# Four gate projections as a double of a seven-product stage, in place of plain chunks ahead of it, with the operand combinations built over half as many steps

## The chip, the cores and the metric

The kernel runs on one core of a Trainium2 chip. A core has a matrix engine (PE, with a separate row PEld for the loading of stationary weights), a vector engine (DVE), a scalar engine (ACT), GpSimd (POOL) and the sync engine (SP), which here only issues transfers. The metric is the device time of one execution in microseconds, as the median of repeated runs. What can be told from no change in this kernel is a difference of about 0.2%, some 2.5 us.

## The reference

One encoder layer on x (512 tokens by 1024 features, float32): a half-step SwiGLU feed-forward, a mixer, and a second half-step feed-forward, each behind an RMSNorm. The mixer projects the normalised input h once and cuts the product apart:

```python
proj = h @ w_in                                   # 1024 x 7936
pa, pq, pk, pv, pg = ...                          # pa: q, k, v of 24 dilated heads; pg: 2 x 1024 gate columns
o_a = dilated attention(pa); o_b = grouped-query attention with rotary(pq, pk, pv)
gates = jax.nn.sigmoid((pg + b_gate).reshape(B, S, N_BRANCHES, D))
merged = gates[:, :, 0] * (o_a @ w_branch_a) + gates[:, :, 1] * (o_b @ w_branch_b)
return merged @ w_out
```

The change touches the first 512 of the 2048 columns of `pg`: four of sixteen gate chunks of 128 columns.

## The kernel before

**Products.** Everything is held feature-major: a tile has 128 features (partitions) by 512 tokens. Each float32 operand is split into a high and a low part in a reduced float32 format (`hH`, `hL` for the normalised input, `wh`, `wl` for weights), and each product is three matmuls (`mm3`, lines 249 to 251: high by high, high by low, low by high). A weight chunk is 128x1024 floats (512 KB): SP loads it raw (`wr`, `wa`, `wt`), ACT rounds it to `wh` (line 234), DVE subtracts to get `wl` (line 235). The rings are short: three `wh`/`wl` pairs, and a fourth (`whx`) for the stage and down-projection items whose index in the order is 3 modulo 4, while a stage pool is open.

**Plain chunks.** `feat` (a gate or a plain q/k chunk) multiplies one weight chunk with all of h: 8 blocks by 3 matmuls, each 512 tokens wide. `token` (the v projections) keeps h stationary and streams the weights. When a gate chunk ends, DVE scales it by the norm factor `R` (line 687) and SP stores it to DRAM (`gate_d`, line 688); it is read back much later, beside the branch products.

**The seven-product stage.** `strassen` takes four chunks at a time (a "double", chunks f and f+1 with both parts) and computes their product with h as a 2x2 block product in seven block products in place of eight. The steps are A11, S1, S2, A12, S3, S4, A22; each is 24 matmuls 256 tokens wide. The right-hand operands of A11, A12 and, in the mixer, S4 are halves of h itself; those of S1, S3, A22 and S2 are combinations of quarters of x that are built beforehand into `TQH`/`TQL` by `tq_steps`: twelve small steps (`put`, `sums`, `part` for each of four k), with two ACT scalings, four DVE combinations of 128x256, one ACT cast (line 734) and one DVE subtraction (line 735) per k. On the weight side A11, A12 (tag `wa`) and A22 (`wr`) are loaded as they are; S1 and S3 (`wt`) are loaded by SP and a second block is added to them by an accumulating transfer from POOL's queue (line 216); S2 and S4 (`ws`) are added by DVE (line 233). Successive doubles overlap by one another's steps: the steps of f+2 begin before those of f end.

**Order around the change.** The PE program order is written out by hand, by `self.items` and the hooks of `project_qk`; on the other engines a scheduler orders the instructions, so they need not stand in the order of the code. The mixer opens with the v projection of group 1 (4 chunks, 32 steps of the generator), then four gate chunks (8 steps each, 64 in all), with the norm statistics at steps 7, 12 and 17 and the twelve `tq_steps` at steps 12, 16, ..., 56. Then comes the stage: five doubles of q/k chunks, whose results go to DRAM (`qk_d`) by POOL's queue, and a sixth double that computes the v projection of group 0. After the stage come the v projection of group 2 and the other plain chunks, woven into the attention; the attention begins by reading q and k back on POOL's queue (`fetch`, line 711).

**Offsets.** Weight tiles of the seven-product steps start at 160 or 32 bytes modulo 256, by the parity of the item's index (`offset`): `return 160 - 128 * (n % 2)`.

Of the kernel before, what the change touches and what calls it, by code (L numbers as in the profile page):

```python
# [20 lines left out]
EARLY, EARLIER = 4, 6  # L21
GROUPS = {"a": (4, 8, 16, 22), "b": (2, 8, 16, 22)}
PAIRS = ((0, 0), (1, 0), (0, 1), (0, 2), (1, 1), (1, 2), (2, 0), (3, 0), (2, 1), (2, 2), (3, 1), (3, 2))
NSQ = 10
STEPS = ("A11", "S1", "S2", "A12", "S3", "S4", "A22")
# [44 lines left out]
class Layer:  # L70
    def __init__(self, ctx, tc, a):
# [27 lines left out]
        gates = lambda lo, hi: [("g", j) for j in range(lo, hi)]  # L99
        self.items = ([("v", 1)] + gates(0, 4) + [("sw", 0), ("v", 2)] + gates(4, 6) + [("qk", f) for f in range(NSQ, 12)]  # L100
                      + gates(6, 13) + [("b", g) for g in range(3)] + gates(13, 16) + [("pa", 0)])
# [3 lines left out]
        for kind, n in self.items:  # L105
            if kind == "sw":
                self.order += [("swq", at) for at in self.slots(range(0, NSQ + 2, 2))]
                continue
            name, m = span[kind]
            self.order += [(name, m * n + i) for i in range(m)]  # L110
        self.order += [(name, i) for name in ("wpb", "wo") for i in range(8)]
        self.order += self.ffn_order("b")
        self.raws, self.tiles, self.used, self.wx, self.TQ = {}, [], 0, None, None
        self.cap = len(self.order)
# [5 lines left out]
    def turn_of(self, n):  # L120
        if self.kind[n] != "wt":
            return n
        s, f = self.order[n][0][2], self.order[n][1][0]
        return n - (EARLIER if s != "q" and f >= GROUPS[s][1] else EARLY)

# [34 lines left out]
    def ring(self, tag, n, done, last):  # L160
        held, bufs = self.rings[tag], BUFS[tag]
        pool = self.wb if tag in ("wr", "wh") else self.wx
        if pool is None or (len(held) >= bufs and held[-bufs] >= done):
            return None
        held.append(last)
        if tag[:2] != "wh":
            return pool.tile([128, 1024], F32, tag=tag, name=tag, bufs=bufs)
        at = (self.offset(n) - BASE[tag]) % 256 // 4
        return tuple(pool.tile([128, 1088], F32R, tag=t, name=t, bufs=bufs)[:, at:at + 1024] for t in ("wh", "wl"))
# [18 lines left out]
    def load(self, n):  # L188
# [17 lines left out]
        def part(q):  # L206
            if name[2] == "q" and f == NSQ:
                return self.a["wav0"][2 * int(q[1]) + int(q[2]) - 3].rearrange("p (a c) -> p a c", a=2)
            i, c = 2 * f + int(q[1]) - 1, 512 * (int(q[2]) - 1)
            return w[i:i + 3:2, :, c:c + 512].rearrange("a p c -> p a c")  # L210

# [89 lines left out]
    def strassen(self, s, fs, evict):  # L301
        st, order = {}, self.slots(fs)
        end = self.used + len(order) - 1
        for f, step in order:
# [7 lines left out]
            for j in range(2):  # L312
                for k in range(4):
                    ops = self.right(step, k)
                    if s == "q" and f == NSQ:
                        ops = [t[:, 128 * j:128 * j + 128] for t in ops] + [t[:, 256 * k:256 * k + 256] for t in cur]
                    else:
                        ops = [t[:, 512 * j + 128 * k:512 * j + 128 * k + 128] for t in cur] + list(ops)
                    self.mm3(ps[:, 256 * j:256 * j + 256], *ops, fresh and j == 0 and k == 0, k == 3, not (fresh and j == 0))
# [115 lines left out]
    def ffn(self, s, gin, gnext, hooks, out=None, side=None):  # L435
        with ExitStack() as ctx:
            pool = lambda n, **k: ctx.enter_context(self.tc.tile_pool(name=n, reuse_waits="tile", **k))
            tp = pool("hT", bufs=1, side="right")
            self.TH = tp.tile([128, 3, 4, 256], F32R, name="TH")
            self.TL = tp.tile([128, 3, 4, 256], F32R, name="TL")  # L440
            self.wx = self.shifted(pool("wx", bufs=1), 128)
            self.cp = self.shifted(pool("c", bufs=2), 128)
            self.ffn_run(s, gin, gnext, hooks, out, side or {}, pool("g", bufs=1))
            self.wx = None
# [294 lines left out]
    def project_qk(self):  # L739
        nc, tc = self.nc, self.tc  # L740
        with ExitStack() as ctx:
            pool = lambda n, **k: ctx.enter_context(tc.tile_pool(name=n, reuse_waits="tile", **k))
            tp = self.shifted(pool("qT", bufs=1), 64)
            self.TQ = [tp.tile([128, 4, 4, 256], F32R, name=f"TQ{c}") for c in "HL"]
            self.wx = self.shifted(pool("wxq", bufs=1), 64)
            cp, qp = pool("cq", bufs=2), pool("qo", bufs=2)
            steps = self.tq_steps(cp)
            hooks = {7: self.stat_r, 12: self.stat_R, 17: self.stat_p}
            for n, _ in enumerate(self.stream(self.items[:self.head])):
                if n in hooks:  # L750
                    hooks[n]()
                if n > 8 and n % 4 == 0 and steps:
                    steps.pop(0)()
# [17 lines left out]
            def store(f, part, t):  # L771
                i = 2 * f + part
                nc.gpsimd.dma_start(self.qk_d[i:i + 3:2].rearrange("c p n -> p c n"), t.rearrange("p (c n) -> p c n", c=2))

# [9 lines left out]
            def evict(f, step, ps):  # L784
# [15 lines left out]
                elif step == "S4":  # L800
                    nc.vector.tensor_add(hi, ps, hi)
                    if f == NSQ:
                        tokens(lo, 0, slice(0, 256), False)
# [5 lines left out]
                    store(f, 0, o)  # L809
                elif f == NSQ:  # L810
                    tokens(ps, 0, slice(256, 512), True)
# [6 lines left out]

            for _ in self.strassen("q", range(0, NSQ + 2, 2), evict):
                pass  # L820
# [498 lines left out]
```

## Time and profile before

| | |
|---|---|
| median of 3 runs | 1253.38 us (1253.02 to 1253.86) |
| the profiled execution | 1252.48 us |
| its span, first to last instruction | 1250.7 us |
| matmul busy (PE) | 1239.0 us, 99% |
| weight loads (PEld) | 1112.9 us, 89% |
| DVE, ACT, POOL busy | 891.4, 595.6, 122.6 us |
| moved by DMA | 183.49 MB, 147 GB/s |
| granted TensorE clock | 0.998 |

The times of the trace are counted from the first instruction of the span; the profiled execution is 1.8 us longer than its span and 0.9 us under the median of the runs. A busy PE is not a PE at its peak, since matmuls are pipelined: the distance from one start to the next tells the pace. The mixer's head (the v projection of group 1 and the four gates) lies between about 348 and 393.5 us, the stage between 393.5 and 508.7 us.

### The profile page before, as it was taken

What the parts mean: (1) busy time and instruction counts of PE and PEld (TensorE: products, weight loads), DVE (VectorE), ACT (ScalarE), POOL (GpSimd) and SP (SyncE); (2) the same over time, 40 slices, a digit from 0 to 9 for tenths busy, and PEclk for the clock granted to TensorE, in tenths of its full rate; (3) what the DMA queues carried; (4) which work ended last, traced back from release to release, by engine and by line L of the source; (5) the groups of instructions that cost most, each with busy time, mean ns of one, the idle gap of its engine ahead of it and who ended that gap; (6) DMA issues with size and microseconds to landing.
All of it is one profiled execution on the core that took longest, in us unless ns stands there. A gap on an engine that the chain in (4) does not pass through costs nothing.

```text
span 1250.7 us, 20135 instructions
## 1 busy us (share of the span) xinstructions
PE 1239.0 (99%) x8076; PEld 1112.9 (89%) x8076; DVE 891.4 (71%) x1344; ACT 595.6 (48%) x886; POOL 122.6 (10%) x128
## 2 busy tenths in 40 slices
PE   9999999999999999999999999999999999999997
PEld 7897999899898999978888878888889989988997
DVE  7784688468784887567745898866678747874874
ACT  8551365245463444454423546654475425532553
POOL 1111101000210210200000200000301001100001
PEclk9999999999999999999999999999999999999999
DMA  9875777241486882762242220157737536743222
GB/s 299 229 193 166 194 194 197 87 119 55 148 209 190 226 236 87 228 186 78 84 141 88 81 93 18 34 155 233 218 101 189 166 101 185 187 151 107 63 85 68
DMA packets 85981, 183.49 MB, mean 147 GB/s; under 512 B 12528, under 2 KB 19072, under 8 KB 85888
## 3 DMA queue, kind: packets, MB, share of 16 engines
q1 hardware_dynamic: 68048, 141.27, 33.7%
q0 software_dynamic: 17120, 40.39, 16.1%
q8 instruction: 63, 1.03, 0.3%
q10 hardware_dynamic: 720, 0.55, 0.1%
q14 instruction: 30, 0.25, 0.1%
HBM read 170.55 MB, written 15.29 MB: 149 GB/s over the span
## 4 chain that ended last, share of the span: by engine, by line
PE 97%; DVE 1%; ACT 1%; DMA 0%; issue 0%; SPq 0%; POOL 0%; DVEq 0%
PE mm L249 25%; PE mm L251 24%; PE mm L250 24%; PE Y L250 4%; PE Y L249 4%; PE Y L251 4%; PE X L250 2%; PE X L251 2%; PE X L249 2%; PE mm L937 1%; PE S L861 1%; PE Tb L1073 1%; PE T L948 1%; PE Sb L251 1%; PE Sb L250 1%; PE Sb L249 1%
## 5 line engine op out<-in xcount | busy, mean ns | idle before, releaser
L234 ACT CAST wh<-wr 128x1024 fp32r<-128x1024 f32 x139 | 145.9, 1049 | 194.7 <-PE mm L250 125.7
L235 DVE TENSOR_TENSOR wl<-wr,wh 128x1024 fp32r<-128x1024 f32 x139 | 169.6, 1221 | 51.5 <-ACT wh L234 51.2
L249 PE MATMUL mm<-hH,wh 128*128 128x256 f32 (+1 forms) x600 | 198.2, 330 | 0.0
L251 PE MATMUL mm<-hH,wl 128*128 128x256 f32 (+1 forms) x600 | 195.4, 326 | 1.0 <-DVE wl L235 1.0
L250 PE MATMUL mm<-hL,wh 128*128 128x256 f32 (+1 forms) x600 | 195.5, 326 | 0.3 <-DVE hL L389 0.3
L249 PE MATMUL mm<-gg,wh 128*128 128x512 f32 (+1 forms) x376 | 141.5, 376 | 0.0
L250 PE MATMUL mm<-gg,wh 128*128 128x512 f32 (+1 forms) x376 | 141.0, 375 | 0.0
L251 PE MATMUL mm<-gg,wl 128*128 128x512 f32 (+1 forms) x376 | 141.0, 375 | 0.0
L251 PEld LDWEIGHTS mm<-hH,wl 128*128 128x128 f32 x600 | 112.9, 188 | 11.8 <-DVE wl L235 1.4
L249 PEld LDWEIGHTS mm<-hH,wh 128*128 128x128 f32 x600 | 112.8, 188 | 11.7 <-issue 1.0
L250 PEld LDWEIGHTS mm<-hL,wh 128*128 128x128 f32 x600 | 113.0, 188 | 10.4 <-DVE hL L389 0.8
L234 ACT CAST wh<-wa 128x1024 fp32r<-128x1024 f32 x50 | 52.6, 1052 | 102.1 <-PE mm L250 55.4
L234 ACT CAST wh<-wt 128x1024 fp32r<-128x1024 f32 x50 | 52.6, 1052 | 71.1 <-PE mm L250 46.4
L235 DVE TENSOR_TENSOR wl<-wt,wh 128x1024 fp32r<-128x1024 f32 x50 | 61.2, 1224 | 33.1 <-ACT wh L234 32.4
L234 ACT CAST wh<-ws 128x1024 fp32r<-128x1024 f32 x50 | 52.6, 1052 | 66.6 <-PE mm L250 47.5
L249 PE MATMUL mm<-TH,wh 128*128 128x256 f32 x304 | 83.9, 276 | 0.0
L250 PE MATMUL mm<-TL,wh 128*128 128x256 f32 x304 | 83.9, 276 | 0.0
L251 PE MATMUL mm<-TH,wl 128*128 128x256 f32 x304 | 83.9, 276 | 0.0
L249 PEld LDWEIGHTS mm<-gg,wh 128*128 128x128 f32 x376 | 70.6, 188 | 14.1 <-PE mm L251 0.9
L251 PEld LDWEIGHTS mm<-gg,wl 128*128 128x128 f32 x376 | 70.6, 188 | 12.9
L250 PEld LDWEIGHTS mm<-gg,wh 128*128 128x128 f32 x376 | 70.6, 188 | 12.6
L545 DVE TENSOR_TENSOR u<-mm,R 128x512 f32<-128x512 f32 x40 | 27.7, 691 | 75.7 <-PE mm L251 75.5
(270 smaller groups left out, 3210.0 us busy)
## 6 DMA issues: line engine op xcount, KB each, us to landing
wr<-in_w2a SPq DMA_DIRECT2D x22, 512.0 KB, 3.4
wr<-in_w2b SPq DMA_DIRECT2D x22, 512.0 KB, 3.5
wt<-in_w13b SPq DMA_DIRECT2D x20, 512.0 KB, 3.5
wa<-in_w13b SPq DMA_DIRECT2D x20, 512.0 KB, 3.3
wt<-in_w13b POOLq DMA_DIRECT2D x20, 512.0 KB, 6.0
wt<-in_w13a SPq DMA_DIRECT2D x18, 512.0 KB, 3.5
wt<-in_w13a POOLq DMA_DIRECT2D x18, 512.0 KB, 6.1
wa<-in_w13a SPq DMA_DIRECT2D x18, 512.0 KB, 3.4
```

Of the source, the lines that this page charges most:

```text
L234: self.nc.scalar.copy(H, raw)
L235: self.nc.vector.tensor_sub(L, raw, f32(H))
L249: mm(out, lH, rH, start=start, stop=False, skip_group_check=more)
L250: mm(out, lH, rL, start=False, stop=False, skip_group_check=more)
L251: mm(out, lL, rH, start=False, stop=stop, skip_group_check=more)
L545: nc.vector.tensor_mul(u, ps, R)
L861: nc.tensor.matmul(*args, start=True, stop=True)
L937: nc.tensor.matmul(oc, v, p, start=st, stop=sp)
L948: nc.tensor.transpose(ps[:, 128 * b:128 * b + 128], P[h][:, c0 + 128 * b:c0 + 128 * b + 128], self.ident)
L1073: nc.tensor.transpose(pt[:, 128 * j:128 * j + 128], P[h, j][:, 128 * k:128 * k + 128], self.ident)
```

## The change

The four leading gate chunks leave the plain stream. They become a double of the stage, number FG = 10, between the last q/k double (f = 8) and the v double, which is renumbered FV = 12; its weights come from `wg` in the same half chunks, and its results are scaled by `R` and stored to `gate_d` by POOL's queue in two transfers of 512 KB. The stage so has seven doubles, 49 steps. Its head has only the v projection of group 1 left, 32 generator steps, and the twelve `tq_steps` are called at steps 8, 10, ..., 30. Two guards are added for loads that would be asked for too early: the turn of the stage's `wt` loads (`turn_of`), and a ring rule that a stage's raw tiles are only taken from that stage's own pool (`self.stage`). The order of items has four fewer gates and seven more steps ahead of everything later, so later items have an index higher by three.

```diff
--- before.py
+++ after.py
@@ -21,7 +21,8 @@
-NSQ = 10
+NSQ, FG, FV = 10, 10, 12
+HEAD_G = 4
 STEPS = ("A11", "S1", "S2", "A12", "S3", "S4", "A22")
...
@@ -97,20 +98,20 @@
-        self.items = ([("v", 1)] + gates(0, 4) + [("sw", 0), ("v", 2)] + gates(4, 6) + [("qk", f) for f in range(NSQ, 12)]
+        self.items = ([("v", 1), ("sw", 0), ("v", 2)] + gates(HEAD_G, 6) + [("qk", f) for f in range(NSQ, 12)]
                       + gates(6, 13) + [("b", g) for g in range(3)] + gates(13, 16) + [("pa", 0)])
         self.head = self.items.index(("sw", 0))
...
-                self.order += [("swq", at) for at in self.slots(range(0, NSQ + 2, 2))]
+                self.order += [("swq", at) for at in self.slots(range(0, FV + 2, 2))]
...
@@ -121,7 +122,9 @@
         s, f = self.order[n][0][2], self.order[n][1][0]
-        return n - (EARLIER if s != "q" and f >= GROUPS[s][1] else EARLY)
+        if s == "q":
+            return max(n - EARLY, self.index["swq", (0, "A11")] - 1)
+        return n - (EARLIER if f >= GROUPS[s][1] else EARLY)
...
@@ -160,7 +163,8 @@
-        if pool is None or (len(held) >= bufs and held[-bufs] >= done):
+        s = self.order[n][0]
+        if pool is None or s[:2] == "sw" and tag != "wh" and s[2] != self.stage or (len(held) >= bufs and held[-bufs] >= done):
             return None
...
@@ -204,10 +208,11 @@
-            if name[2] == "q" and f == NSQ:
+            if name[2] == "q" and f == FV:
                 return self.a["wav0"][2 * int(q[1]) + int(q[2]) - 3].rearrange("p (a c) -> p a c", a=2)
-            i, c = 2 * f + int(q[1]) - 1, 512 * (int(q[2]) - 1)
-            return w[i:i + 3:2, :, c:c + 512].rearrange("a p c -> p a c")
+            src, i = (self.a["wg"], 0) if name[2] == "q" and f == FG else (w, 2 * f)
+            i, c = i + int(q[1]) - 1, 512 * (int(q[2]) - 1)
+            return src[i:i + 3:2, :, c:c + 512].rearrange("a p c -> p a c")
...
@@ -742,14 +747,14 @@
-                if n > 8 and n % 4 == 0 and steps:
+                if n > 6 and n % 2 == 0 and steps:
                     steps.pop(0)()
...
@@ -769,8 +774,8 @@
-                i = 2 * f + part
-                nc.gpsimd.dma_start(self.qk_d[i:i + 3:2].rearrange("c p n -> p c n"), t.rearrange("p (c n) -> p c n", c=2))
+                dst, i = (self.gate_d, part) if f == FG else (self.qk_d, 2 * f + part)
+                nc.gpsimd.dma_start(dst[i:i + 3:2].rearrange("c p n -> p c n"), t.rearrange("p (c n) -> p c n", c=2))
...
@@ -816,7 +821,7 @@
-            for _ in self.strassen("q", range(0, NSQ + 2, 2), evict):
+            for _ in self.strassen("q", range(0, FV + 2, 2), evict):
                 pass
             self.wx = self.TQ = None
```

The scheduler's order moves with it (the same statements stand five or so lines further down in the changed kernel: L735 becomes L740). The first place is DVE at the end of the v projection of group 1. `TQL` is the low part of the combinations, `Traw` their raw form, `ws` a weight sum (S2 or S4), `wl` the low part of a weight chunk, `V1` the evicted v projection, `z` an evicted gate. Before:

```order
L726 SCALAR_TENSOR_TENSOR Traw_3727<-Traw_3727 128x256
L235 TENSOR_TENSOR wl_3764<-ws_3765,wh_3763 128x1024
L735 TENSOR_TENSOR TQL_3450<-Traw_3666,TQH_3449 128x1024
L667 TENSOR_SCALAR V1_3444<-mm_3462,r_90 128x512
L726 SCALAR_TENSOR_TENSOR Traw_3727<-Traw_3727 128x256
L233 TENSOR_TENSOR ws_3926<-ws_3765,wa_3559 128x1024
L735 TENSOR_TENSOR TQL_3450<-Traw_3727,TQH_3449 128x1024
L233 TENSOR_TENSOR ws_3967<-wt_3556,wa_3561 128x1024
L235 TENSOR_TENSOR wl_3567<-wr_3469,wh_3566 128x1024
L667 TENSOR_SCALAR V1_3444<-mm_3464,r_90 128x512
L235 TENSOR_TENSOR wl_3646<-wr_3510,wh_3645 128x1024
L687 TENSOR_TENSOR z_3678<-mm_3644,R_91 128x512
```

With the change:

```order
L731 SCALAR_TENSOR_TENSOR Traw_3641<-Traw_3641 128x256
L238 TENSOR_TENSOR ws_3790<-ws_3575,wa_3474 128x1024
L672 TENSOR_SCALAR V1_3442<-mm_3460,r_90 128x512
L740 TENSOR_TENSOR TQL_3448<-Traw_3613,TQH_3447 128x1024
L731 SCALAR_TENSOR_TENSOR Traw_3641<-Traw_3641 128x256
L238 TENSOR_TENSOR ws_3831<-wt_3471,wa_3476 128x1024
L740 TENSOR_TENSOR TQL_3448<-Traw_3641,TQH_3447 128x1024
L240 TENSOR_TENSOR wl_3570<-wt_3463,wh_3569 128x1024
L672 TENSOR_SCALAR V1_3442<-mm_3462,r_90 128x512
L240 TENSOR_TENSOR wl_3668<-wa_3474,wh_3667 128x1024
L240 TENSOR_TENSOR wl_3700<-wa_3476,wh_3699 128x1024
```

What stood there between the combinations were the low parts of two gate chunks (`wr`) and then the gates' evictions; now the sum for S4 of the first double stands ahead of an eviction, the sum for S2 of the second (`ws_3831`) stands ahead of the last `TQL`, and the low parts of S1 (`wl_3570`), A12 and the next A11 follow at once.

The second place is SP's queue, from the last load of the v projection on. `wr<-in_wg` is a gate chunk, `wt` the first block of S1 or S3, `wa` A11 or A12, `wr<-in_waq` A22. Before:

```order
L201 DMA wr_3359<-in_wg 128x1024
L215 DMA wt_3471<-in_waq 128x2x512
L213 DMA wa_3551<-in_waq 128x2x512
L201 DMA wr_3469<-in_wg 128x1024
L215 DMA wt_3553<-in_waq 128x2x512
L215 DMA wt_3556<-in_waq 128x2x512
L201 DMA wr_3510<-in_wg 128x1024
L213 DMA wa_3559<-in_waq 128x2x512
L213 DMA wa_3561<-in_waq 128x2x512
L215 DMA wt_3563<-in_waq 128x2x512
L201 DMA wr_3549<-in_wg 128x1024
```

With the change:

```order
L218 DMA wr_3481<-in_waq 128x2x512
L220 DMA wt_3463<-in_waq 128x2x512
L218 DMA wa_3466<-in_waq 128x2x512
L220 DMA wt_3468<-in_waq 128x2x512
L220 DMA wt_3471<-in_waq 128x2x512
L218 DMA wa_3474<-in_waq 128x2x512
L218 DMA wa_3476<-in_waq 128x2x512
L220 DMA wt_3478<-in_waq 128x2x512
L218 DMA wr_3799<-in_waq 128x2x512
L218 DMA wr_4030<-in_waq 128x2x512
L218 DMA wa_3582<-in_waq 128x2x512
```

The four gate loads, three of which stood between the first loads of the stage, are gone, and the next A22, A11 and S1 loads have moved up behind them.

The third place is POOL's queue at the end of the stage: `qk_d<-qo` stores a q/k half double, `qk<-qk_d` reads one back for the attention. Before:

```order
L773 DMA qk_d_114<-qo_4758 128x2x512
L773 DMA qk_d_114<-qo_4819 128x2x512
L773 DMA qk_d_114<-qo_4979 128x2x512
L773 DMA qk_d_114<-qo_5042 128x2x512
L711 DMA qk_5193<-qk_d_114 128x512
L711 DMA qk_5195<-qk_d_114 128x512
```

With the change:

```order
L778 DMA qk_d_114<-qo_4853 128x2x512
L778 DMA qk_d_114<-qo_4914 128x2x512
L778 DMA gate_d_113<-qo_5076 128x2x512
L778 DMA gate_d_113<-qo_5139 128x2x512
L716 DMA qk_5288<-qk_d_114 128x512
L716 DMA qk_5290<-qk_d_114 128x512
```

Two gate stores now stand between the last q/k store and the first read.

More of the change, by code (lines that the diff above doesn't have):

```diff
@@ L112, in __init__ @@
         self.order += self.ffn_order("b")
-        self.raws, self.tiles, self.used, self.wx, self.TQ = {}, [], 0, None, None
+        self.raws, self.tiles, self.used, self.wx, self.TQ, self.stage = {}, [], 0, None, None, None
         self.cap = len(self.order)
@@ L314, in strassen @@
                     ops = self.right(step, k)
-                    if s == "q" and f == NSQ:
+                    if s == "q" and f == FV:
                         ops = [t[:, 128 * j:128 * j + 128] for t in ops] + [t[:, 256 * k:256 * k + 256] for t in cur]
@@ L440, in ffn @@
             self.TL = tp.tile([128, 3, 4, 256], F32R, name="TL")
-            self.wx = self.shifted(pool("wx", bufs=1), 128)
+            self.wx, self.stage = self.shifted(pool("wx", bufs=1), 128), s
             self.cp = self.shifted(pool("c", bufs=2), 128)
@@ L744, in project_qk @@
             self.TQ = [tp.tile([128, 4, 4, 256], F32R, name=f"TQ{c}") for c in "HL"]
-            self.wx = self.shifted(pool("wxq", bufs=1), 64)
+            self.wx, self.stage = self.shifted(pool("wxq", bufs=1), 64), "q"
             cp, qp = pool("cq", bufs=2), pool("qo", bufs=2)
@@ L801, in evict @@
                     nc.vector.tensor_add(hi, ps, hi)
-                    if f == NSQ:
+                    if f == FV:
                         tokens(lo, 0, slice(0, 256), False)
@@ L809, in evict @@
                     store(f, 0, o)
-                elif f == NSQ:
+                elif f == FV:
                     tokens(ps, 0, slice(256, 512), True)
```

## The prediction

> **What bounds the kernel now.** I read the page first (parts 1 and 4), then a table of stretches around the place of the change, then the timelines of PE, DVE and ACT there.
>
> ```profile
> span 1250.7 us, 20135 instructions
> PE 1239.0 (99%) x8076; PEld 1112.9 (89%) x8076; DVE 891.4 (71%) x1344; ACT 595.6 (48%) x886; POOL 122.6 (10%) x128
> PE 97%; DVE 1%; ACT 1%; DMA 0%; issue 0%; SPq 0%; POOL 0%; DVEq 0%
> ```
>
> The chain that ended last is matmuls for 97% of the span. So the time is the number of matmuls times their pace, plus whatever new wait the change puts in front of one. The table of stretches (PE, PEld, DVE, ACT, POOL busy with counts, clock, DMA share, GB/s) shows what lies beside the matmuls:
>
> ```profile
> 346.00:371.70 25.70, 25.70 (x117) 25.16 (x116) 23.04 (x37) 17.05 (x22) 4.77 (x4) 1.00 0.84 225
> 371.70:393.50 21.80, 21.80 (x98) 18.02 (x96) 8.66 (x9) 4.23 (x5) 0.00 (x0) 1.00 0.60 179
> 418.20:437.20 19.00, 19.00 (x170) 19.00 (x169) 16.03 (x18) 8.82 (x10) 3.58 (x4) 1.00 0.93 249
> 437.20:456.30 19.10, 19.10 (x171) 19.10 (x170) 16.58 (x19) 8.82 (x10) 3.76 (x5) 1.00 0.89 246
> ```
>
> The first row is the v projection at the head of the mixer: DVE is busy for 23.04 of 25.70 us. The second is the four gates, where DVE does little (8.66 of 21.80). The others are one double of the stage each. PE is full in all of them, and the clock is whole. The change takes out the second row and adds one more of the last kind, so the first row now meets the stage directly.
>
> **What is removed, and what is added.** The starts of PE and ACT give both:
>
> ```profile
> 371.71 0.39 PE L249 MATMUL mm<-hH,wh 128*128 128x512 f32 x1
> 393.50 0.28 PE L249 MATMUL mm<-hH,wh 128*128 128x256 f32 x1
> 396.33 0.28 PE L249 MATMUL Y<-TQH,wh 128*128 128x256 f32 x1
> 427.39 0.58 ACT L791 COPY c<-mm 128x512 f32<-128x512 f32 x1
> 465.47 0.58 ACT L791 COPY c<-mm 128x512 f32<-128x512 f32 x1
> 480.75 0.28 PE L249 MATMUL mm<-wh,hH 128*128 128x256 f32 x1
> 508.72 0.52 PE L249 MATMUL mm<-wh,hH 128*128 128x512 f32 x1
> ```
>
> The first gate matmul starts at 371.71, the first of the stage at 393.50: the four gates hold PE for 21.79 us, or 227 ns for each of 4 x 24 = 96 matmuls. A double's first product is evicted (ACT, line 791) at 427.39, and two doubles later at 465.47: 38.08 / 2 = 19.04 us per double, 2.72 us for each of 7 steps, 113.3 ns for each of 168 matmuls. A matmul of half the width so costs half, and seven products in place of eight save an eighth: 19.04 - 21.79 = **-2.75 us**.
>
> The Trainium skill speaks against as much gain: TensorE: Matmul & The Clock Gate, section Back-to-back issue gap, gives an isolated warm gap of N/2.4 + 2.5 ns, so 215.8 ns at 512 and 109.2 ns at 256 columns; by that, an estimate, the sum is 168 x 0.1092 - 96 x 0.2158 = -2.37 us. Both rows here are slower than the formula (227 and 113.3 ns), in one proportion, and the row decides.
>
> The pace of a step has two values, which sets the bounds of this term. The first step of the stage takes 393.50 to 396.33, 2.83 us, and the last ten, where the last q/k double and the v double alternate, take 508.72 - 480.75 = 27.97 us, 0.77 us more than ten at 2.72. At 0.11 us each that is seven of the ten. The trace gives no cause. If the added double ran at the pace of the first step throughout, it would take 7 x 2.83 = 19.81 us and the sum would be -1.98. If, at the other end, the ten last steps changed to 2.72 (their weight offsets flip parity, since the v double now begins at an even index), the sum would be -2.75 - 0.77 = -3.52. I take -2.75, the pace of the steps between. The later index shift of three flips the offsets of the second feed-forward as well; each of its three stage entries may then gain or lose one slow step, 2.83 - 2.72 = 0.11 us, so at most 0.33 in all; I take none.
>
> **What is moved: the combinations.** These are the rows of DVE, ACT and POOL at the end of the v projection, before the change:
>
> ```profile
> 354.41 1.22 DVE L235 TENSOR_TENSOR wl<-wr,wh 128x1024 fp32r<-128x1024 f32 x1
> 355.55 2.35 DVE L735 TENSOR_TENSOR TQL<-Traw,TQH 128x1024 fp32r<-128x1024 f32 x2
> 361.04 0.43 DVE L728 TENSOR_TENSOR Traw<-Traw 128x256 f32<-128x256 f32 x1
> 361.38 1.23 DVE L235 TENSOR_TENSOR wl<-wr,wh 128x1024 fp32r<-128x1024 f32 x1
> 366.28 0.75 DVE L667 TENSOR_SCALAR V<-mm,r 128x512 f32<-128x512 f32 x1
> 366.95 0.41 DVE L726 SCALAR_TENSOR_TENSOR Traw<-Traw 128x256 f32<-128x256 f32 x1
> 367.45 1.05 ACT L734 CAST TQH<-Traw 128x1024 fp32r<-128x1024 f32 x1 [2.37 <-DVE Traw L726]
> 368.53 1.23 DVE L735 TENSOR_TENSOR TQL<-Traw,TQH 128x1024 fp32r<-128x1024 f32 x1
> 370.51 1.05 ACT L234 CAST wh<-wr 128x1024 fp32r<-128x1024 f32 x1 [0.72 <-PE mm L251]
> 371.59 1.23 DVE L235 TENSOR_TENSOR wl<-wr,wh 128x1024 fp32r<-128x1024 f32 x1 [0.69 <-ACT wh L234]
> 356.71 1.20 POOL L216 DMA_DIRECT2D wt<-in_waq  x1 [0.55 <-DMA wt<-in_waq]
> DMA to landing us min/median/max: 3.3/5.9/10.5
> ```
>
> The important thing is that the last `TQL` already ends at 368.53 + 1.23 = 369.76, ahead of the first gate: the scheduler had not spread the build over the gates, although the code offered it 64 steps. So halving the cover takes away room that was not used. I walk through DVE's new order with these distances (1.14 from one 128x1024 row to the next, 0.34 for a combination). From 355.55: `TQL`, `ws`, `TQL` to 358.97; the copy to `acc` (0.55) and one combination to 359.86; `wl` of S2 and A11 to 362.14; a small copy and six combinations to 364.3; the sum for S4 to 365.4. The eviction waits for its bank as before, 366.28, and ends at 366.95; then `TQL` to 368.1, one combination to 368.4, the sum for S2 of the next double to 369.6, the last `TQL` (its cast runs 368.4 to 369.5) to 370.8. The low part of S1 follows the cast at 370.51, whose slot PE frees late, and ends at 371.59 + 1.23 = 372.82, where a gate chunk's stood before.
>
> When are they needed? A11 is first on PE, at 371.71, and its `wl` is there at 362.1. S1 is the first to read `TQ`, one slow step later: 371.71 + 2.83 = 374.54. So the combinations are 3.7 us early and the weights of S1 1.7 us early: **cost 0**. What hides them is the A11 step itself, which touches neither. With that cover gone, S1 would wait 372.82 - 371.71 = 1.1 us. From then on each step frees a weight slot 2.72 us before the next, as inside the stage, where DVE keeps up with 16.03 to 16.58 us per 19.04.
>
> **What is moved: transfers.** SP loses four gate loads of 512 KB and four stores of 256 KB, and gains five loads; POOL gains two accumulating loads and two stores of 512 KB. The rows that tell whether the loads of the stage come in time:
>
> ```profile
> 394.22 1.20 POOL L216 DMA_DIRECT2D wt<-in_waq  x1 [23.41 <-DMA wt<-in_waq]
> 421.00 1.05 ACT L234 CAST wh<-wt 128x1024 fp32r<-128x1024 f32 x1 [1.18 <-PE mm L250]
> 498.87 0.73 POOL L773 DMA_DIRECT2D qk_d<-qo  x1 [3.86 <-DVE qo L767]
> 509.19 4.29 POOL L711 DMA_DIRECT2D qk<-qk_d  x8 [9.59 <-PE mm L251]
> ```
>
> The fifth accumulating load (S1 of the third double) is issued at 394.22 and read at 421.00, and that reader waits for PE, not for DMA. With the change it is read 21.79 us sooner, at 399.2; its slot comes free at 372.82, and even two transfers of the longest landing above (10.5) with POOL's 1.2 between end by 395.0. A double moves as before from then on, at a DMA share of 0.89 to 0.93. Cost 0; the cover is the ring, two doubles deep. On POOL the two gate stores stand ahead of the reads of q and k, but the last store is issued some 10 us before the end of the stage (498.87 against 508.72), and the reads wait 9.59 us for PE anyway: 0, and with that wait gone 2 x 0.73 us of issue.
>
> **The sum** is -2.75 us: 1250.7 - 2.75 = 1247.95 of span, 1252.48 - 2.75 = 1249.7 for the profiled execution. That execution lies 0.9 us under the median of 1253.38, so the median becomes **1250.6 us**, -0.22%, only just past the 0.2% (2.5 us) that a measurement can tell from no change.
>
> **The rivals.** (A) The added double runs slowly: -1.98, so 1251.4, no change that can be told. For it: the first step and seven of the last ten were slow. Against: the added double lies in the middle of the stage, and the two doubles from 427.39 to 465.47 show no slow step. (B) The tail speeds up: -3.52, 1249.9. For it: the slow steps stand where the v double alternates, and by the code its offsets flip. Against: no row shows the new pairing. (C) A short wait at the entry: DVE comes later than in my walk by more than the 1.7 us of S1, for instance because the cast waits longer for its slot. With two more rows of 1.14 us ahead of it 2.3 - 1.7 = 0.6 us are lost, with four 4.6 - 1.7 = 2.9: 1251.2 to 1253.5, in the middle 1252.3. (D) Slower: the sum for S2 of the second double (`ws<-wt,wa`) now stands in DVE's queue ahead of the last `TQL` and S1's `wl`, and it waits for POOL's accumulating load issued at 356.71. Landing by 356.71 + 10.5 = 367.2, with the longest of the `wt` landings between 338 and 400 us, it is in time. Behind the sum come 3 x 1.14 us of DVE, so PE waits once it lands after 374.54 - 3.42 = 371.1, and the gain is gone from 373.9 on. The load after it shows that this can be (POOL's issue of its second block, and SP's issues of the first blocks):
>
> ```profile
> 369.61 1.20 POOL L216 DMA_DIRECT2D wt<-in_waq  x1 [11.70 <-DMA wt<-in_waq]
> 350.09 0.94 SPq L215 DMA_DIRECT2D wt<-in_waq  x2
> 357.03 0.73 SPq L215 DMA_DIRECT2D wt<-in_waq  x1
> ```
>
> Its first block took from 357.03 to 369.61, 12.6 us. Were both transfers of S1 so slow (issued as the second of the two at 350.09, so at some 350.6; then 12.6, POOL's 1.2, 12.6), it would land at 377.0: 5.9 us of wait, 1250.6 + 5.9 = 1256.5, 0.25% slower. Against: three gate loads that stood between these loads are gone. (E) Half-wide matmuls are bound by their weight loads: PEld is busy for all of 19.00 us in the stage. If each took its 188 ns, the double would hold PE for 31.6 us, and the time would be 1263.2. Five doubles already show 113.3 ns, so I give it under 1 in 100. The sustained spacing in the Trainium skill, TensorE: Matmul & The Clock Gate, section Back-to-back issue gap (81 ns at 128 columns, 131 ns at 512) would point that way; the 227 ns here do not fit it.
>
> ```profile
> L249 PEld LDWEIGHTS mm<-hH,wh 128*128 128x128 f32 x600 | 112.8, 188 | 11.7 <-issue 1.0
> ```
>
> **Chances.** The forecast 0.50, A 0.17, B 0.12, C 0.12, D (with E) 0.09. The forecast's own spread, 0.33 us for the feed-forward and as much for two medians, leaves about a fifth of it short of 2.5 us. So faster: 0.50 x 0.8 + 0.12 = 0.52; slower: 0.09; no change: 0.39. The range reaches from B less its 0.3, 1249.6, to the upper part of C, 1253.2, and leaves D out.
>
> **What would show it.** Right: the first matmul on `TQ` 2.8 us after the end of the v projection with no wait for DVE, 49 steps of 2.72 to 2.83 us, and the first 512-wide matmul behind them at 508.72 - 2.75 = 506.0. Wrong: a PE wait on `TQL`, `wl` or `ws` near 374 (C, D), PE starts 118 ns apart in the gate double (A), or an ACT or DVE wait for `wt` by DMA inside the stage.

## The result, and the profile after

The changed kernel takes 1251.09 us in the median of 16 runs (1250.49 to 1252.72); the kernel before, on the same chip, 1253.3 us (1252.1 to 1255.38). The ratio is 0.9983, with a 95% interval of 0.9976 to 0.9991: faster by 0.17%, just short of the 0.2% that the prediction took for the least that can be told; the interval reaches past it. The forecast was 1250.6 us, in a range of 1249.6 to 1253.2. So the time was nearly met, and the span shows that this is not the whole story: it fell by 1.4 us where the sum had said 2.75. The medians fell by 2.2 us. The profiled execution of the kernel before (1252.48) was 0.8 us faster than its median, that of the changed kernel (1251.12) was at its own; so a single span is good to about a microsecond, and what follows sets the two traces against each other place by place. The page of the changed kernel, its first lines and the first line of the chain that ended last:

```profile
span 1249.3 us, 20296 instructions
PE 1236.4 (99%) x8148; PEld 1113.7 (89%) x8148; DVE 902.6 (72%) x1352; ACT 599.4 (48%) x892; POOL 126.7 (10%) x132
PE 94%; DVE 3%; ACT 1%; POOL 0%; issue 0%; DMA 0%; SPq 0%; DVEq 0%; POOLq 0%
```

PE has 72 matmuls more (168 for 96) and is busy for 2.6 us less. In the chain that ended last, though, PE has lost three points, and DVE has two more. I looked first at the place of the change: PE's timeline at the stage's entry and at its end (start, duration, engine, line, operation), and DVE's timeline at the entry.

```profile
371.61 0.40 PE L256 MATMUL mm<-wh,hL 128*128 128x512 f32 x1
371.84 0.28 PE L254 MATMUL mm<-hH,wh 128*128 128x256 f32 x1
374.67 0.28 PE L254 MATMUL Y<-TQH,wh 128*128 128x256 f32 x1
506.05 0.51 PE L254 MATMUL mm<-wh,hH 128*128 128x512 f32 x1
```

```profile
369.80 1.23 DVE L740 TENSOR_TENSOR TQL<-Traw,TQH 128x1024 fp32r<-128x1024 f32 x1
371.71 1.23 DVE L240 TENSOR_TENSOR wl<-wt,wh 128x1024 fp32r<-128x1024 f32 x1 [0.69 <-ACT wh L239]
```

The first narrow matmul follows the last wide one after 0.23 us, without a wait. From there to the first 512-wide matmul behind the stage it takes 506.05 - 371.84 = 134.21 us; before the change, from the first gate matmul, 508.72 - 371.71 = 137.01. The place of the change gives back 2.80 us, all that was forecast. The loss comes later. The waits of PE, summed by what it waited for (us in total, times, longest), have one row that is new in size. First of the kernel before, then of the changed one:

```profile
PE Tb L1073 <- DVE Pb L1067: 0.2, 1, 0.2
```

```profile
PE Tb L1078 <- DVE Pb L1072: 1.3, 1, 1.3
```

It is one transposition, at the start of the second attention part, where DVE normalises the score rows `Pb` that PE transposes. PE's timeline there, before and after:

```profile
741.85 0.33 PE L1073 MATMUL Tb<-ident,Pb 128*128 128x128 f32 x1 [0.15 <-DVE Pb L1067]
```

```profile
740.67 0.33 PE L1078 MATMUL Tb<-ident,Pb 128*128 128x128 f32 x1 [1.32 <-DVE Pb L1072]
```

With the starts of all matmuls set against each other one by one, the changed kernel is 2.4 to 2.6 us ahead up to this row and 1.2 behind it. Some 0.15 us more goes in the second feed-forward. So 2.7 us were won in the stage, and half of that was lost 235 us later, at a line that the diff doesn't touch. Why DVE is late there, its own timeline shows (the low parts `wl` of the weight chunks, and the first row maximum `nm` of the attention), before and after:

```profile
709.89 1.21 DVE L235 TENSOR_TENSOR wl<-wr,wh 128x1024 fp32r<-128x1024 f32 x1
720.49 1.22 DVE L235 TENSOR_TENSOR wl<-wr,wh 128x1024 fp32r<-128x1024 f32 x1
729.68 1.22 DVE L235 TENSOR_TENSOR wl<-wr,wh 128x1024 fp32r<-128x1024 f32 x1
732.62 1.21 DVE L235 TENSOR_TENSOR wl<-wr,wh 128x1024 fp32r<-128x1024 f32 x1
735.00 0.68 DVE L1062 TENSOR_REDUCE nm<-Sb 128x1 f32<-128x512 f32 x1
727.60:737.60 10.00, 10.00 (x49) 8.20 (x48) 9.21 (x16) 4.01 (x8) 0.00 (x0) 1.00 0.48 157
```

```profile
717.89 1.22 DVE L240 TENSOR_TENSOR wl<-wr,wh 128x1024 fp32r<-128x1024 f32 x1
726.69 1.22 DVE L240 TENSOR_TENSOR wl<-wr,wh 128x1024 fp32r<-128x1024 f32 x1
729.69 1.22 DVE L240 TENSOR_TENSOR wl<-wr,wh 128x1024 fp32r<-128x1024 f32 x1
732.62 1.23 DVE L240 TENSOR_TENSOR wl<-wr,wh 128x1024 fp32r<-128x1024 f32 x1
734.35 1.29 DVE L1067 TENSOR_REDUCE nm<-Sb 128x1 f32<-128x512 f32 x2
725.00:735.00 10.00, 10.00 (x49) 8.20 (x48) 10.00 (x17) 2.45 (x4) 0.00 (x0) 1.00 0.46 162
```

Before, two low parts stand in the last 9 us ahead of the first `nm`, and a third was made long before, at 709.89. After, all three stand there, and DVE is busy for all of the 10 us; before, in the same stretch (it lies 2.6 us later there), it was busy for 9.21 (the last line of each, a row of the table of stretches: PE, PEld, DVE, ACT, POOL busy, granted clock, DMA share, GB/s). With a lead of 2.6 us the first `nm` should start at 732.4; it starts at 734.35.

The code has one thing that moves a single chunk so. Each chunk's high and low part go into a ring of slots `wh`/`wl`, and a chunk whose index leaves the remainder 3 by four, in the projection of the second attention (`wb`) and in the seven-product stages, gets a slot of its own ring, `whx`, where one is open (method `prep`). The change makes the list of chunks longer by three behind the stage (seven steps for four gates). The four chunks of a `wb` group had the indices 160 to 163, and the last of them got the extra slot; now they have 163 to 166, and the first one gets it. (The description of the kernel before names only the stage and the down-projection for this slot; the line in `prep` has `"wb"` as well.) By the code, a chunk that loses the slot has to wait for an ordinary one.

### The profile page after: what moved, and what is told of

Same layout as the page of the kernel before. It is cut to its first block, busy times and chain, and to the rows that moved or that the text cites. A ratio compares the mean times of both kernels' runs of the same rounds, so it can differ in the third digit from the quotient of the medians.

```text
span 1249.3 us, 20296 instructions
## 1 busy us (share of the span) xinstructions
PE 1236.4 (99%) x8148; PEld 1113.7 (89%) x8148; DVE 902.6 (72%) x1352; ACT 599.4 (48%) x892; POOL 126.7 (10%) x132
## 4 chain that ended last, share of the span: by engine, by line
PE 94%; DVE 3%; ACT 1%; POOL 0%; issue 0%; DMA 0%; SPq 0%; DVEq 0%; POOLq 0%
PE mm L254 24%; PE mm L256 24%; PE mm L255 23%; PE Y L256 4%; PE Y L254 4%; PE Y L255 4%; PE X L256 2%; PE X L254 2%; PE X L255 2%; PE mm L942 1%; PE S L866 1%; PE Tb L1078 1%; PE T L953 1%; DVE wl L240 0%; PE Sb L256 0%; PE Sb L255 0%
## 5 line engine op out<-in xcount | busy, mean ns | idle before, releaser
L239 ACT CAST wh<-wr 128x1024 fp32r<-128x1024 f32 x136 | 142.6, 1049 | 193.3 <-PE mm L255 128.0
L240 DVE TENSOR_TENSOR wl<-wr,wh 128x1024 fp32r<-128x1024 f32 x136 | 166.6, 1225 | 51.2 <-ACT wh L239 50.9
L254 PE MATMUL mm<-hH,wh 128*128 128x256 f32 (+1 forms) x576 | 187.7, 326 | 0.3 <-ACT hH L393 0.3
L256 PE MATMUL mm<-hH,wl 128*128 128x256 f32 (+1 forms) x576 | 185.0, 321 | 1.0 <-DVE wl L240 1.0
L255 PE MATMUL mm<-hL,wh 128*128 128x256 f32 (+1 forms) x576 | 185.0, 321 | 0.3 <-DVE hL L394 0.3
L254 PEld LDWEIGHTS mm<-hH,wh 128*128 128x128 f32 x576 | 108.3, 188 | 11.1 <-issue 1.0
L256 PEld LDWEIGHTS mm<-hH,wl 128*128 128x128 f32 x576 | 108.2, 188 | 10.6 <-DVE wl L240 1.5
L255 PEld LDWEIGHTS mm<-hL,wh 128*128 128x128 f32 x576 | 108.3, 188 | 9.1 <-DVE hL L394 0.8
L240 DVE TENSOR_TENSOR wl<-wt,wh 128x1024 fp32r<-128x1024 f32 x52 | 63.7, 1224 | 34.1 <-ACT wh L239 33.4
```

The source lines that it names most:

```text
L239: self.nc.scalar.copy(H, raw)
L240: self.nc.vector.tensor_sub(L, raw, f32(H))
L254: mm(out, lH, rH, start=start, stop=False, skip_group_check=more)
L255: mm(out, lH, rL, start=False, stop=False, skip_group_check=more)
L256: mm(out, lL, rH, start=False, stop=stop, skip_group_check=more)
```

## Experiments

Two theories stood against the one just told (T1, the index shift): that the loss comes from the stage's earlier end itself, as DVE's work on q and k doesn't come earlier with it (T2), and that it belongs to the second feed-forward, whose weight offsets flip with the index (T3).

### The old slots in the changed kernel, the new slots in the kernel before

In the changed kernel, the remainder is taken as before the change for `wb` alone:

```
-  ... in ("sw", "w2", "wb") and n % 4 == 3 and ...
+  ... in ("sw", "w2", "wb") and (n + 1 * (self.order[n][0] == "wb")) % 4 == 3 and ...
```

In the kernel before, the same line has `n + 3 * (...)`, which gives `wb` the slots that it has in the changed kernel, and nothing else is altered.

> The changed kernel, but the attention projection's items (wb) get their fourth slot whx at the chunks that had it before the change (the last chunk of each group in place of the first). Theory 1 (the index shift by three moved the slot, so the low parts of later chunks reach DVE's queue in the saturated stretch ahead of attention B, and PE waits there for Pb): the wait of Tb for Pb near 740 us falls from 1.3 us to about 0.2 as before the change, and the whole lead of 2.6 us is kept to the end: span about 1248.1, 1.2 us under the changed kernel, 2.6 under the kernel before. Theory 2 (the loss comes from the stage's earlier end itself: DVE's work on q and k does not end earlier because its transfers do not): the wait stays at 1.3 us, span 1249.3. Theory 3 (the loss belongs to the second feed-forward's parity flip): the wait stays, span 1249.3, since that flip is kept here.

> The kernel before, with only the slot choice of the attention projection's items shifted as the change shifts it (whx for the first chunk of each group). Theory 1: the wait of Tb for Pb at the start of the second attention part grows from 0.2 to about 1.3 us, and the span from 1250.7 to about 1251.9. Theory 2 or 3: nothing moves, 1250.7, wait 0.2.

The row of the wait in both, first the changed kernel with the old slots, then the kernel before with the new ones:

```profile
PE Tb L1078 <- DVE Pb L1072: 0.2, 1, 0.2
```

```profile
PE Tb L1073 <- DVE Pb L1067: 1.3, 1, 1.3
```

The wait goes with the slots and with nothing else: 0.2 us in the changed kernel with the old slots, 1.3 in the old kernel with the new slots. In the starts of the matmuls, 1.2 us come back at this place in the one and are lost in the other. T2 and T3 have both fallen as the reason for it.

The whole times say the same, less sharply. The changed kernel with the old slots takes 1250.2 us, ratio 0.9977 (0.9967 to 0.9987) to the kernel before; the old kernel with the new slots 1254.23 against 1252.77, ratio 1.0007 (0.9998 to 1.0016). The intervals are nearly as wide as the effect, so the verdict rests on the row. The span of the first, 1248.9, missed the 1248.1 expected: in the execution that was profiled, PE waited 1.2 us instead of 0.7 for DVE's `MX` near 573 us and ended the first attention part 1.0 us later. The next kernel, which has the same order up to the second feed-forward, doesn't show this. The span of the second, 1252.6, is 0.7 above the 1251.9 expected; 0.4 of that was lost in its first 18 us, far from the edit.

### The old index for everything behind the stage

The remainder of `wb` and of the second feed-forward, and the parity that sets the second feed-forward's weight offsets, are taken by the old index:

```
-            return 160 - 128 * (n % 2)
+            return 160 - 128 * ((n + (name == "swb")) % 2)
...
+  ... (n + (self.order[n][0] in ("wb", "swb", "w2b"))) % 4 == 3 ...
```

> The changed kernel with the old index in all that counts by it behind the stage: the slot choice of wb, and the slot choice and the offset parity of the second feed-forward. Theory 1 with the parity rule for slow steps (a stage of the feed-forward that starts at an odd offset has two slow steps, at an even one has one): as the run with the slot choice of wb alone, and 0.1 to 0.2 us less behind the second feed-forward, four slow steps there instead of five: span about 1248.0. Theory 3: nearly all of the 1.4 us comes back here and nothing in the run with the slots of wb alone. Theory 2: 1249.2.

```profile
span 1247.8 us, 20299 instructions
PE Tb L1078 <- DVE Pb L1072: 0.2, 1, 0.2
732.40 0.68 DVE L1067 TENSOR_REDUCE nm<-Sb 128x1 f32<-128x512 f32 x1
```

The first `nm` is back at 732.40. The span is 1247.8, 2.9 us under the kernel before, and from the first wide matmul behind the stage to the last of the kernel the lead over the kernel before stays at 2.72 us to within 0.15. That is the sum of the prediction, with every other edit at nothing. In the second feed-forward four steps are slow, five with the new parity: 0.11 us of the 0.15 lost there. The median is 1249.58 us, ratio 0.9973 (0.9960 to 0.9985). By the trace it beats the changed kernel by 1.5 us; the two intervals overlap.

### How much room there is at the entry

The prediction put the combinations 3.7 us and the weights of S1 1.7 us ahead of their use. The rows above give 374.67 - (369.80 + 1.23) = 3.6 and 374.67 - (371.71 + 1.23) = 1.7. To see whether these are the limits, some work is done several times over, which leaves the output the same. First the last low part of `TQ`, three times:

```
-            nc.vector.tensor_sub(L, raw[k], f32(H))
+            for _ in range(3 if k == 3 else 1):
+                nc.vector.tensor_sub(L, raw[k], f32(H))
```

> The changed kernel, where the last subtraction that builds TQ's low part is done three times over (same output), 2.28 us more of DVE's time ahead of the low part of S1. It measures the entry's margins, forecast at 3.7 us for the combinations and 1.7 us for the weights of S1. By the walk: TQ's last low part ends at 373.1 and stays in time, the low part of S1 ends at about 375.1 and S1 waits about 0.6 us near 374.5; span 1249.9. If the margin were all slack (more than 2.3 us): no wait, 1249.3. If the entry were already at its edge: a wait of up to 2.3 us.

DVE's timeline there, and the first matmul of PE that reads this last low part:

```profile
369.77 2.49 DVE L741 TENSOR_TENSOR TQL<-Traw,TQH 128x1024 fp32r<-128x1024 f32 x2
372.17 1.22 DVE L240 TENSOR_TENSOR wl<-wt,wh 128x1024 fp32r<-128x1024 f32 x1
373.31 1.22 DVE L741 TENSOR_TENSOR TQL<-Traw,TQH 128x1024 fp32r<-128x1024 f32 x1
375.82 0.28 PE L255 MATMUL Y<-TQL,wh 128*128 128x256 f32 x1
```

The scheduler put the third one behind S1's low part. So the combinations end at 373.31 + 1.22 = 374.53, 3.5 us later than in the changed kernel, and PE doesn't wait. S1 starts at 374.64, but this isn't the limit: the repeated low part is that of the last of four blocks (`k == 3`), S1 takes the blocks in order, and by the code its eleventh matmul, at 375.82, is the first that reads it. So 1.3 us are left, and the margin of the combinations is 375.85 - 371.03 = 4.8 us in the changed kernel, not 3.6; no run here reaches its end. The expected 0.6 us didn't come, since the order that it assumed wasn't the one built; the span is 1249.2, as the changed kernel's (1249.3), and the median 1251.39 (ratio to the kernel before 0.9986, 0.9977 to 0.9995).

Then S1's own low part, four times and three times, on the kernel with the old index (the line stands in `prep`):

```
-        self.nc.vector.tensor_sub(L, raw, f32(H))
+        for _ in range(4 if (name, key) == ("swq", (0, "S1")) else 1):
+            self.nc.vector.tensor_sub(L, raw, f32(H))
```

> The changed kernel with the old index throughout, where the subtraction that makes the low part of S1's weights (first double of the stage) is done four times over, same output. The repeats stand among V's eviction and the next low part on DVE. By the rows of the changed kernel the first begins at 371.71 and the last would end at 371.71 + 5 x 1.14 + 0.67 + 1.23 - 1.14 = 378.2 (four of these, one other low part, V's eviction). S1's third matmul wants it at 374.67 + 0.24 = 374.9. If that is the limit, as the prediction's walk has it: a PE wait for wl of about 3.3 us at S1, span about 1247.8 + 3.3 = 1251.1. If there is slack that the walk missed (S1 needs its low part later, or the stage catches up): less, down to 1247.8.

> As the run in which the low part of S1 was made four times, but three times. In that run PE waited 4.3 us and then ran 24 matmuls at half its clock, 2.4 us more. Here the last repeat starts at 375.66 by that run's rows and ends at 376.9, so PE waits 376.9 - 374.8 = 2.1 us. If the clock falls only after a longer wait: span 1247.8 + 2.1 = 1249.9. If any wait of some us brings it: 2.4 more, 1252.3.

The wait of PE, and the table of stretches around it (PE, PEld, DVE, ACT, POOL busy with counts, granted clock, DMA share, GB/s), four times:

```profile
PE Y L257 <- DVE wl L241: 4.3, 1, 4.3
374.50:379.20 4.70, 0.44 (x5) 0.23 (x3) 4.64 (x5) 1.53 (x2) 0.00 (x0) 0.84 0.36 116
379.20:384.50 5.30, 5.30 (x25) 5.30 (x26) 0.00 (x0) 0.37 (x1) 0.34 (x1) 0.50 0.58 195
```

and three times:

```profile
PE Y L257 <- DVE wl L241: 2.0, 1, 2.0
377.10:380.60 3.50, 3.48 (x17) 3.48 (x18) 1.10 (x1) 0.00 (x0) 0.00 (x0) 0.53 0.86 281
```

The third matmul of S1, the first that reads the low part, does wait for it: the walk's limit is the real one, to the 0.24 us from S1's first matmul to its third. The wait is 1 us longer than expected with four, as one more low part stood between the repeats. What the walk didn't have is the second row. After 4.3 us without work PE runs for 5.3 us at a clock of 0.50, and after 2.0 us it runs for 3.5 us at 0.53. The lead falls by 6.8 us for a wait of 4.3, and by 3.7 for one of 2.0 (spans 1254.9 and 1251.6 against 1247.8; the first has a median of 1256.32, ratio 1.0029, 1.0018 to 1.0039, the second was executed once). Of the two cases that were set out for the shorter wait, the one in which the clock falls is right. The wait of 1.3 us at `Tb` in the changed kernel brought no such stretch: the clock is 1.00 on both sides of it.

### A second double of gates

Gates 4 to 7 follow the first four into the stage as one more double (`FG = (10, 12)`, `FV = 14`, `HEAD_G = 8`), with the old slots behind it. The filler of the attention parts loses these four gates; the third rope group keeps two of three, and its first transposition comes after three pieces of filler instead of six (`rope_t(2, 3, 4)`).

> Two doubles of gates in place of one (gates 0 to 7 in the stage, the v double behind both), with the old slot choice for the items behind. The four further gates leave the filler between the attention parts, so the third rope group has two gates of cover instead of three, and its first transposition comes after three pieces of filler instead of six. Theory 1 (the sum of the prediction holds per double, and nothing else is at its limit): 2.75 us less than the run with the old index throughout, span about 1245.1, ratio to the kernel before about 0.995. Rival (the cover is needed where it was taken): three pieces of filler are 3 x 0.68 = 2 us, and PE waits up to that much for the rope rows or for Pb at the start of the second attention part: 1245.1 to 1247.8, so that the second double brings little or nothing.

```profile
span 1251.3 us, 20461 instructions
PE T L953 <- DVE MX L874: 2.5, 4, 1.6
PE Tb L1078 <- DVE Pb L1072: 0.9, 1, 0.9
PE mm L255 <- DVE PTL L160: 0.8, 3, 0.4
```

The second double makes the stage 19.09 us longer, for 21.8 of gates, 2.7 less, and yet the span is 3.5 us longer than with one, 1251.3; the median is 1252.9, ratio 0.9999 (0.9989 to 1.0008). That is worse than the rival's 1247.8. The gates that went were work under which PE waited for nobody. PE stands still for 5.0 us between 535 and 930 us, against 1.5 us between 516 and 930 with one double (the gaps of the tables of stretches, added up), 3.5 us more: for the row maxima of the first attention part (2.5 for 0.7), for `Pb` (0.9 for 0.2), for the split of the transposed rows. Some 2.6 us more are missing from the gain that was expected, and they are not in rows of waits. They lie in the pace of the attention's own matmuls: added up from each start to the next, without the waits, the transposes (`T`, `Tb`) take 1.1 us longer than with one double, the value products (`PTH`, `PTL`) 0.8 and the score products (`S`, `Sb`) 0.5. Why they are slower, the runs don't show.

### What makes a step slow

The prediction left open why some steps take 2.83 instead of 2.72 us. Each chunk's slot begins at one of two offsets (160 and 32 bytes, modulo 256), in turn from step to step. On the kernel with the old index, once the two are exchanged in the stage, once the stage has one only (160), and once all seven-product steps have one, the feed-forwards too (`return 160`). The stage has 49 steps, not the 56 that two of the expectations say; by 49, the case of all steps slow would cost 4.5 us instead of 5.3.

> The changed kernel with the old index throughout, and the two weight offsets of the stage exchanged for all 56 steps. If the slow steps (2.83 instead of 2.72 us) go by the offset: one slow step at the entry in place of two, and seven instead of six at the end, as before the change: same time within 0.1 us. If they go by the data or the step's kind: the same steps as without the exchange.

> The changed kernel with the old index throughout, and one offset for all weights of the stage in place of two in turn. If the slow pace comes from a step whose weights lie at another offset than the next one's, the slow steps vanish: eight less, -0.9 us, span 1246.9. If it comes from two neighbours at the same offset, all 56 steps are slow: 48 more x 0.11 = +5.3 us, span 1253.1. If the offset has nothing to do with it: 1247.8.

> The same kernel as the one-offset run (old index behind the stage, one weight offset for the whole stage), timed in rounds, to tell whether it beats the changed kernel and the one with the old index. By the steps of its one profile, four slow steps of the stage in place of eight, 0.45 us, with the entry's two among those gone: median about 1249.1, ratio to the kernel before 0.997. If the offset has a cost elsewhere that one profile doesn't show: as the old index with two offsets, 1249.6.

> The old index behind the stage, and one weight offset for the seven-product steps of all stages, the two feed-forwards too. If one offset is never worse than two: the slow steps of the feed-forwards fall from seven to six or fewer (none at the entries would be -0.8 us), span 1247.3 to 1246.5. If the exchange of offsets protects the feed-forwards' steps, 150 steps of 0.11 us can be lost: up to 1263.

PE's timeline at the first and second step of the stage with the offsets exchanged:

```profile
371.56 0.28 PE L254 MATMUL mm<-hH,wh 128*128 128x256 f32 x1
374.29 0.28 PE L254 MATMUL Y<-TQH,wh 128*128 128x256 f32 x1
```

With one offset everywhere, the starts of two neighbouring steps of the first feed-forward, of a later A11 step there and its successor, and of an A11 step of the mixer's stage and its successor:

```profile
56.05 0.28 PE L254 MATMUL Y<-TH,wh 128*128 128x256 f32 x1
58.88 0.28 PE L254 MATMUL mm<-TH,wh 128*128 128x256 f32 x1
64.53 0.28 PE L254 MATMUL mm<-hH,wh 128*128 128x256 f32 x1
67.36 0.28 PE L254 MATMUL mm<-hH,wh 128*128 128x256 f32 x1
446.38 0.28 PE L254 MATMUL mm<-hH,wh 128*128 128x256 f32 x1
449.10 0.28 PE L254 MATMUL mm<-TQH,wh 128*128 128x256 f32 x1
```

Exchanged, the entry's first step takes 374.29 - 371.56 = 2.73 where the changed kernel's takes 2.83; neither of the first two steps is slow now, where I expected one, and seven at the end are, as expected (span 1247.3, one execution). With one offset in the stage none is slow at the entry and four at the end, four in place of eight, which is none of the three cases set out; the spans are 1247.6 and 1247.2. The medians can't tell this from the two offsets: 1250.08 us, ratio 0.9976 (0.9967 to 0.9985), against 0.9973. With one offset everywhere all 133 steps of the feed-forwards are slow, 58.88 - 56.05 = 2.83: span 1262.6, median 1263.32, ratio 1.0084 (1.0071 to 1.0097), the loss that was expected if the exchange protects them. So the feed-forwards need the exchange, and the stage of the mixer doesn't.

A step's own addresses don't decide it. By the addresses that the built program gives its tiles, the A11 step at 64.53 and the one at 446.38 read the same slots of weights and the same parts of `hH` and `hL`, matmul by matmul; the first takes 67.36 - 64.53 = 2.83, the second 449.10 - 446.38 = 2.72. So what ran before a step counts. In the kernel before, the changed one, the old index, the two doubles and the first two offset runs, 40 of the 42 stages begin with a slow step. In each of the 40 the slow pace ends at the first step with weights at 32 that follows a step at 160: one slow step where the stage begins at 160, two where it begins at 32. With 160 throughout, the feed-forwards begin slow and never leave it, and the mixer's stage, which begins fast at 160, stays fast. At that stage's end, where the v double with the operands' roles turned alternates with the last double ahead of it, four to seven steps are slow in every case. What in the sequence of addresses makes the slow pace, the runs don't settle.

## Why the prediction was right

**The sum.** Right, to 0.05 us. The stage with one more double and no gates takes 2.80 us less from its first to its last row (forecast 2.75), and with the old index behind it this lead stays to the end. The doubles follow each other at 19.04 us, as the rows before had it. The estimate of -2.37 worked out by the Trainium skill, TensorE: Matmul & The Clock Gate, section Back-to-back issue gap, is too small by 0.4. Its two gaps lie under the measured ones by unequal shares (215.8 for 227 ns, 109.2 for 113.3), not in one proportion.

**The entry.** Right: cost 0. The walk gave 370.8 for the end of the last low part of `TQ` and 372.82 for S1's; measured are 371.03 and 372.94, and S1 starts at 374.67 (forecast 374.54). The two runs with repeated low parts of S1 show that this one is the limit. For the combinations the walk took too early a need: their last block is first read by S1's eleventh matmul, 1.2 us after its start, and the run with the third `TQL` shows only that 3.5 us of delay fit in. Rival C, a short wait there, didn't come. Its price, the lateness itself, would have been too low at 2.0 us, the shortest wait here after which the clock fell; so would rival D's 5.9.

**The pace.** The entry's first two steps are slow in both kernels (the prediction had seen the first only), and six at the end are, instead of seven: one slow step less, 0.1 us, by which -2.75 becomes -2.85, and -2.80 was measured. Neither A (the added double slow) nor B (the end faster) came. That the flipped offsets matter in the second feed-forward was right in kind, at most 0.33, measured about 0.1.

**The transfers.** PE, ACT and DVE have no wait for a DMA inside the stage, as forecast; POOL has some ahead of its accumulating loads, as before the change. Rival D didn't come.

**The step that failed** is the sentence on the index: "The later index shift of three flips the offsets of the second feed-forward as well". It stops there. The same index picks the extra slot, for the attention's projection `wb` too, so the shift also moved one weight chunk's low part of 1.2 us into the stretch of DVE ahead of the second attention part, where DVE is full, and PE paid 1.2 us for it. Nothing in the walk looked at DVE there; the only place of the change that was walked was its own. Without this step the forecast of the span would have been met to 0.15 us (1247.95 against 1247.8). With it, the span was 1249.3, and the median of 1251.09 lies 0.5 us above the forecast. That it is inside the range is luck: the range's width came from other rivals, none of which happened.

## What to carry to other kernels

When an edit changes the length of a list, look at every choice that is made by the index, modulo something: slots, parities, engines. A table of instructions per engine, old against new, shows such a moved instruction far from the edit, and the stretch into which it moves has to be read like the edit's own. And work that looks slow by itself may be the cover of something else: the same exchange that won 2.7 us in front of the attention made the kernel 3.5 us longer when the gates were taken from between its waits.

## What the runs showed of the hardware

A wait costs more than its length once PE has been without work for about 2 us here. After 2.0 us it ran 17 matmuls in 3.5 us at a granted clock of 0.53, and after 4.3 us 25 matmuls in 5.3 us at 0.50; after 1.3 us (`Tb` in the changed kernel) and 1.6 us (`T` with two doubles of gates) nothing of the kind. The Trainium skill, TensorE: Matmul & The Clock Gate, section HAM oscillation — how this bites in real kernels, gives gaps of more than about 3.4 us as what to avoid. The 2.0 us here were enough, each length having been tried once.

The same 24 matmuls, in the same order, with the same shapes and the same addresses of both operands, take 2.72 or 2.83 us by what ran before them. A slow pace at the entry of a stage went on until a step with weights at offset 32 followed one at 160 (40 entries in six runs); without such a step it lasted through all 133 steps of the feed-forwards, which cost 14 us.
